# Five low weight parts made by ScalarE and an accumulating DMA in place of VectorE

## The chip, the cores and the metric

The kernel runs on one core of one Trainium2 chip. The metric is the device time of one execution in microseconds. The times of before are a median over 3 runs. Beside them stands one profiled execution, from which all rows below come.

## The reference, cut to what matters

The reference is a trunk of two layers over 512 tokens of width 1024. Layer 0 mixes with an S5 state-space layer, layer 1 with sparse attention, and each is followed by a SwiGLU feed-forward layer. The change lies in layer 0's mixer:

```
y = Re(C state) + D * u
y = gelu(y)
val, gate = split(y @ w_glu, 2)        # w_glu: 1024 x 2048
x = x + val * sigmoid(gate)
```

All of it is in float32. The kernel reaches this precision with three matmuls for each product: every operand is split into a rounded high part and a low part (the rest), and high times high, high times low and low times high are added in PSUM.

## The kernel before, in words

`wblock` fetches one block of weights: SP loads it to `w_raw` (line 262), ScalarE (ACT) copies it rounded to `w_hi` (line 263), and VectorE (DVE) writes the low part `w_lo` = `w_raw` - `w_hi` (line 265). `w_raw` has 2 buffers, `w_hi` and `w_lo` 3 each, shared by all layers.

The S5 layer works through its 64 channel groups in 8 rounds, `u` = 0 to 7. In a round VectorE makes tables (lines 666 to 671), the readout `VV` (lines 801 to 803, one buffer) and the scan with its rotations (lines 769 to 784, result `X`). TensorE (PE) transposes, and adds two products into `acc`: line 811, which needs `M` (filled from `Kd` by up to 8 small DMAs, line 717), and line 812, which needs `VV` and `X`. ACT applies GELU (line 817), PE transposes the result (line 825), and ACT and VectorE split it into the high and low part of `y[u]` (lines 830 and 831). GpSimd (POOL) only clears the first column of `X` in this stage (line 764).

Beside the rounds TensorE begins the projection `y @ w_glu` as a filler: 16 partial blocks (`glu_parts`, matmuls at lines 272 to 274 with high, high and low weights) take the `y[k]` that exist already. Every partial sum is copied out by ACT (`part`, line 873). The 16 blocks have 2, 2, 3, 3, 3, 3, 4, 4, 4, 4, 5, 5, 6, 6, 7 and 7 row tiles; neighbours are fetched together in 11 groups (`refill`). The first five groups hold two blocks each: 128x512, 128x768, 128x768, 128x1024 and 128x1024 elements. Groups 0 and 1 are fetched at the end of round 0. When all rounds are done, `glu_sum` computes the rest of the projection, and the feed-forward layer follows.

The order of each engine's instructions comes from a planner, which goes by program order as priority and by simulated readiness. Until the first `refill`, VectorE and ACT are under a manual schedule (line 432, closed at line 960). Each engine runs its instructions in the planned order, so an instruction that waits holds up those behind it.

Of the kernel before, what the change touches and what calls it, by code (L numbers as in the profile page):

```python
# [15 lines left out]
AF = mybir.ActivationFunctionType  # L16
ALU = mybir.AluOpType
# [3 lines left out]
P = 128  # L21
D = 1024
# [183 lines left out]
class Trunk:  # L206
# [47 lines left out]
    def wblock(self, src, nk, cols, lo_engine=None):  # L254

        nc = self.nc
        raw_t = self.wp.tile([P, KT * P], F32, name="w_raw", bufs=2)
        hi_t = self.wp.tile([P, KT * P], F32R, name="w_hi", bufs=3)
        lo_t = self.wp.tile([P, KT * P], F32R, name="w_lo", bufs=3)
        raw, hi, lo = (t[:, : nk * cols] for t in (raw_t, hi_t, lo_t))  # L260
        v = "p (k c) -> p k c"
        nc.sync.dma_start(out=raw.rearrange(v, k=nk), in_=src)
        nc.scalar.activation(hi, raw, AF.Copy)  # L263
        if lo_engine is None:
            nc.vector.tensor_tensor(lo, raw, hi, op=ALU.subtract)  # L265
        else:
            lo_engine.tensor_tensor(lo, raw, hi, op=ALU.subtract)  # L267
        return hi.rearrange(v, k=nk), lo.rearrange(v, k=nk)
# [98 lines left out]
    def s5(self, gain_row, x_ap, lre, lim, ldt, b_re, b_im, c_re, c_im, d_ap, w_glu):  # L367
        nc, tc = self.nc, self.tc
        V, PL, AC, PE = nc.vector, nc.gpsimd, nc.scalar, nc.tensor
        ident = self.ident  # L370
        wg = w_glu.rearrange("(k p) f -> p k f", p=P)
# [465 lines left out]
        cuts = [u for u in range(UN) for _ in range(GLU_BLOCKS[u])]  # L837
        cut.update(zip(order, cuts))
        groups, n = [], 0
        while n < len(order):  # L840
            m = n + 1
# [3 lines left out]
            n = m  # L845
        ready, done = {}, [0]
        fetched = [0]

        def refill(ahead):
            while fetched[0] < min(len(groups), done[0] + ahead):  # L850
                n, m = groups[fetched[0]]
                fetched[0] += 1
                d, i = order[m - 1]
                whi, wlo = self.wblock(wg[:, 0 : cuts[n], i * D + d * P : i * D + (d + m - n) * P], cuts[n], (m - n) * P)
                for b in range(n, m):
                    c = slice((m - 1 - b) * P, (m - b) * P)
                    ready[b] = whi[:, :, c], wlo[:, :, c]
# [67 lines left out]
        for u in range(UN):  # L925
# [30 lines left out]
            if more:  # L956
                ES[u + 1] = turns_out(u + 1, E[u + 1])
            refill(3 if u else 2)
            if u == 0:
                manual.close()  # L960
# [440 lines left out]
```

## Time and profile before

| | |
|---|---|
| median of 3 runs | 1294.6 us (1293.08 to 1294.64) |
| the profiled execution | 1290.61 us |
| its span, first to last instruction | 1288.9 us |
| mean granted TensorE clock | 0.993 |
| PE busy in the span | 1227.3 us (95%) |
| DVE busy | 764.7 us (59%) |
| ACT busy | 547.4 us (42%) |
| POOL busy | 147.9 us (11%) |

A share over the whole span is a mean over stages. The S5 rounds take about the first 186 us; the stage table among the rows below is the place to read for this change.

### The profile page before, as it was taken

The numbers are of one execution on the slowest core, as the hardware profiler recorded it, in microseconds if no ns is written. First come the engines' busy times: TensorE is split into PE (matmuls) and PEld (weight loads), VectorE is DVE, ScalarE is ACT, GpSimd is POOL, SyncE is SP. The second block draws the span as 40 slices with busy tenths as digits, with TensorE's granted clock in tenths as the row PEclk, the third lists the DMA queues.
The fourth block names the chain that finished last, engine by engine and source line by source line (L and its number), as shares of the span: only waits on it lengthen the run. The fifth ranks groups of instructions, "written<-read, shape, count | busy, mean of one in ns | idle before, by whom it ended". The sixth has DMA issues, their size and how long they took to land.

```text
span 1288.9 us, 18063 instructions
## 1 busy us (share of the span) xinstructions
PE 1227.3 (95%) x6844; PEld 1051.0 (82%) x6844; DVE 764.7 (59%) x1533; ACT 547.4 (42%) x1234; POOL 147.9 (11%) x174
## 2 busy tenths in 40 slices
PE   4589999999999999999989899999999999999998
PEld 4467778888888888889989799988888888888887
DVE  8999958654444443334899976775754444443221
ACT  7755445433332322322573778865532322232221
POOL 1000000000000000005754444510000000000000
PEclk9999999999999999999989999999999999999999
DMA  5021234333333333333213111111433333333341
GB/s 121 10 83 47 65 90 124 98 98 99 98 98 98 99 90 95 101 95 95 74 42 99 60 41 34 42 34 50 123 98 98 98 98 98 98 91 94 112 117 45
DMA packets 189735, 108.02 MB, mean 84 GB/s; under 512 B 7208, under 2 KB 188560, under 8 KB 189584
## 3 DMA queue, kind: packets, MB, share of 16 engines
q1 hardware_dynamic: 189264, 106.70, 28.5%
q8 instruction: 54, 0.88, 0.3%
q14 instruction: 33, 0.27, 0.1%
q10 hardware_dynamic: 384, 0.16, 0.1%
HBM read 102.39 MB, written 2.10 MB: 81 GB/s over the span
## 4 chain that ended last, share of the span: by engine, by line
PE 77%; DVE 5%; ACT 2%; issue 1%; DMA 1%; POOL 0%; ACTq 0%; DVEq 0%; POOLq 0%
PE acc L272 21%; PE acc L274 21%; PE acc L273 21%; PE acc L1062 8%; PE acc L1267 2%; PE tr L1256 1%; DVE ro L999 1%; PE lg L1240 1%; DVE pe L1243 1%; DVE mask L1170 1%; PE lg L1239 0%; DVE kl L1117 0%; PE tr L1099 0%; DVE m L1169 0%; ACT pe L1246 0%
## 5 line engine op out<-in xcount | busy, mean ns | idle before, releaser
L263 ACT ACTIVATE w_hi<-w_raw 128x1024 fp32r<-128x1024 f32 (+5 forms) x208 | 199.9, 963 | 512.9 <-PE acc L273 467.6
L265 DVE TENSOR_TENSOR w_lo<-w_raw,w_hi 128x1024 fp32r<-128x1024 f32 (+6 forms) x179 | 194.0, 1085 | 142.5 <-ACT w_hi L263 141.1
L272 PE MATMUL acc<-h,w_hi 128*128 128x512 f32 x704 | 274.5, 390 | 0.0
L274 PE MATMUL acc<-h,w_lo 128*128 128x512 f32 x704 | 273.9, 389 | 0.0
L273 PE MATMUL acc<-h,w_hi 128*128 128x512 f32 x704 | 273.7, 389 | 0.0
L1062 PE MATMUL acc<-w_hi,h 128*128 128x256 f32 (+1 forms) x896 | 174.7, 292 | 0.8 <-ACT h L284 0.8
L273 PEld LDWEIGHTS acc<-h,w_hi 128*128 128x128 f32 x704 | 132.2, 188 | 27.9 <-issue 0.5
L272 PEld LDWEIGHTS acc<-h,w_hi 128*128 128x128 f32 x704 | 132.2, 188 | 27.6 <-issue 0.5
L274 PEld LDWEIGHTS acc<-h,w_lo 128*128 128x128 f32 x704 | 132.2, 188 | 27.6
L1062 PEld LDWEIGHTS acc<-w_hi,h 128*128 128x128 f32 x896 | 141.4, 192 | 1.4 <-ACT h L284 1.0
L1062 PE MATMUL acc<-w_lo,h 128*128 128x256 f32 (+1 forms) x448 | 126.9, 288 | 0.3 <-POOL w_lo L267 0.3
L339 DVE TENSOR_TENSOR u<-acc,rinv 128x512 f32<-128x512 f32 x44 | 30.4, 690 | 132.4 <-PE acc L274 132.4
L272 PE MATMUL acc<-f,w_hi 128*128 128x512 f32 x272 | 106.4, 391 | 0.0
L274 PE MATMUL acc<-f,w_lo 128*128 128x512 f32 x272 | 105.9, 389 | 0.0
L273 PE MATMUL acc<-f,w_hi 128*128 128x512 f32 x272 | 105.8, 389 | 0.0
L1062 PEld LDWEIGHTS acc<-w_lo,h 128*128 128x128 f32 x448 | 85.2, 192 | 0.9 <-POOL w_lo L267 0.5
L336 DVE TENSOR_TENSOR g<-acc,rinv 128x512 f32<-128x512 f32 x44 | 30.4, 691 | 85.5 <-PE acc L274 85.5
L267 POOL TENSOR_TENSOR w_lo<-w_raw,w_hi 128x1024 fp32r<-128x1024 f32 (+2 forms) x29 | 69.5, 2408 | 49.9 <-ACT w_hi L263 49.8
L274 PEld LDWEIGHTS acc<-f,w_lo 128*128 128x128 f32 x272 | 51.1, 188 | 10.6
L273 PEld LDWEIGHTS acc<-f,w_hi 128*128 128x128 f32 x272 | 51.1, 188 | 10.5
L272 PEld LDWEIGHTS acc<-f,w_hi 128*128 128x128 f32 x272 | 51.1, 188 | 10.4
L272 PE MATMUL acc<-y,w_hi 128*128 128x512 f32 x128 | 51.1, 406 | 2.8 <-ACT y L830 1.1
(296 smaller groups left out, 1981.3 us busy)
## 6 DMA issues: line engine op xcount, KB each, us to landing
w_raw<-in_ffn_w_gate_up_dram SPq DMA_DIRECT2D x88, 512.0 KB, 3.7
w_raw<-in_ffn_w_down_dram SPq DMA_DIRECT2D x32, 448.0 KB, 3.7
w_raw<-in_dsa_w_in_dram SPq DMA_DIRECT2D x26, 512.0 KB, 3.5
w_raw<-in_ffn_w_down_dram SPq DMA_DIRECT2D x16, 512.0 KB, 3.8
w_raw<-in_dsa_w_o_dram SPq DMA_DIRECT2D x16, 256.0 KB, 2.8
w_raw<-in_s_w_glu_dram SPq DMA_DIRECT2D x6, 384.0 KB, 3.5
xc<-in_x_dram SPq DMA_DIRECT2D x8, 256.0 KB, 5.7
xr<-in_x_dram SPq DMA_DIRECT2D x4, 512.0 KB, 3.5
```

The lines of the kernel that those rows point to most:

```text
L263: nc.scalar.activation(hi, raw, AF.Copy)
L265: nc.vector.tensor_tensor(lo, raw, hi, op=ALU.subtract)
L267: lo_engine.tensor_tensor(lo, raw, hi, op=ALU.subtract)
L272: mm(out, lhsT=whi, rhs=xx[:, 0], start=start, stop=False)
L273: mm(out, lhsT=whi, rhs=xx[:, 1], start=False, stop=False)
L274: mm(out, lhsT=wlo, rhs=xx[:, 0], start=False, stop=stop)
L336: nc.vector.tensor_tensor(g, ps[0], rinv, op=ALU.mult)
L339: nc.vector.tensor_tensor(u, ps[1], rinv, op=ALU.mult)
L999: nc.vector.tensor_tensor(out, a, b, op=ALU.add)
L1062: PE.matmul(pt[:, :n], lhsT=h[k][:, l, ts], rhs=ww, start=(k == 0 and i == 0), stop=(k == KT - 1 and i == 2))
L1170: V.match_replace(out=sc, in_to_replace=m8, in_values=sc, imm_value=GONE)
L1267: PE.matmul(po[s, b][:, i * HD : (i + 1) * HD], lhsT=pT[:, j * P : (j + 1) * P], rhs=vv[j][:, (s * 4 + i) * HD : (s * 4 + i + 1) * HD], st ...
```

## The change

For the first five groups the low part is made in two steps in place of one. ACT writes minus the high part to `w_lo`, and a DMA that GpSimd issues adds the weights from DRAM to it. VectorE no longer takes part, and `w_raw` is read by ACT alone. The other six groups, `glu_sum` and the other layers keep the subtraction.

```diff
@@ wblock
         nc.scalar.activation(hi, raw, AF.Copy)
-        if lo_engine is None:
+        if lo_engine == "dma":
+            nc.scalar.activation(lo, hi, AF.Copy, scale=-1.0)
+            nc.gpsimd.dma_start(out=lo.rearrange(v, k=nk), in_=src, accum_op=ALU.add)
+        elif lo_engine is None:
             nc.vector.tensor_tensor(lo, raw, hi, op=ALU.subtract)
@@ refill
                 n, m = groups[fetched[0]]
+                lo = "dma" if fetched[0] < 5 else None
                 fetched[0] += 1
                 d, i = order[m - 1]
-                whi, wlo = self.wblock(wg[...], cuts[n], (m - n) * P)
+                whi, wlo = self.wblock(wg[...], cuts[n], (m - n) * P, lo)
```

## Rows read from the trace of the kernel before

**Rows 1.** Busy time (share of the span) and instructions of each engine, from the page

```profile
PE 1227.3 (95%) x6844; PEld 1051.0 (82%) x6844; DVE 764.7 (59%) x1533; ACT 547.4 (42%) x1234; POOL 147.9 (11%) x174
```

**Rows 2.** Windows: length, busy PE, PEld, DVE, ACT, POOL; PE clock; DMA share; GB/s

```profile
66.00:74.70 8.70, 7.73 (x68) 6.20 (x67) 8.64 (x16) 4.70 (x12) 0.00 (x0) 0.77 0.45 131
74.70:82.00 7.30, 6.01 (x61) 5.06 (x61) 7.27 (x15) 3.37 (x6) 0.00 (x0) 1.00 0.16 40
82.00:98.50 16.50, 13.95 (x113) 11.21 (x107) 16.41 (x31) 8.31 (x19) 0.11 (x1) 1.00 0.27 76
98.50:150.00 51.50, 51.10 (x376) 41.40 (x377) 50.84 (x96) 27.79 (x59) 0.33 (x3) 1.00 0.20 54
150.00:186.00 36.00, 33.99 (x242) 27.47 (x240) 22.18 (x39) 11.72 (x19) 0.52 (x3) 1.00 0.32 87
```

**Rows 3.** Timeline of DVE: start, duration, line, operation [idle before, releaser]

```profile
66.41 1.55 DVE L265 TENSOR_TENSOR w_lo<-w_raw,w_hi 128x512 fp32r<-128x512 f32 x2
67.88 0.68 DVE L771 TENSOR_TENSOR z<-z,z 128x512 f32<-128x512 f32 x1
...
77.01 0.95 DVE L265 TENSOR_TENSOR w_lo<-w_raw,w_hi 128x768 fp32r<-128x768 f32 x1
77.87 0.68 DVE L770 TENSOR_TENSOR z<-lg,ES 128x512 f32<-128x512 f32 x1
...
79.81 0.68 DVE L801 TENSOR_TENSOR VV<-Cst,hC 128x512 f32<-128x512 f32 x1
...
90.07 1.22 DVE L265 TENSOR_TENSOR w_lo<-w_raw,w_hi 128x1024 fp32r<-128x1024 f32 x1
91.20 1.72 DVE L784 TENSOR_TENSOR X<-z,z 64x252 f32<-64x252 f32 x4
...
104.96 1.22 DVE L265 TENSOR_TENSOR w_lo<-w_raw,w_hi 128x1024 fp32r<-128x1024 f32 x1
```

**Rows 4.** Timeline of PE around its idle gaps

```profile
72.22 0.62 PE L811 MATMUL acc<-M,U 128*64 128x128 f32 x4
...
73.34 0.40 PE L274 MATMUL acc<-y,w_lo 128*128 128x512 f32 x1
74.67 0.40 PE L812 MATMUL acc<-VV,X 128*64 128x128 f32 x2 [0.93 <-DVE X L784]
...
78.59 0.71 PE L825 MATMUL tr<-ident,yg 64*128 64x64 f32 x8 [0.68 <-ACT yg L817]
...
90.05 0.50 PE L272 MATMUL acc<-y,w_hi 128*128 128x512 f32 x1 [0.86 <-ACT part L873]
...
92.61 0.40 PE L812 MATMUL acc<-VV,X 128*64 128x128 f32 x2 [0.90 <-DVE X L784]
```

**Rows 5.** Timeline of ACT around the high parts

```profile
63.53 1.34 ACT L263 ACTIVATE w_hi<-w_raw 128x512 fp32r<-128x512 f32 x2
64.78 0.40 ACT L756 ACTIVATE ES<-E 128x256 f32<-128x256 f32 x1
...
66.78 0.60 ACT L680 ACTIVATE WT<-tr 128x512 f32<-128x512 f32 x1 [1.29 <-PE tr L679]
...
88.47 1.04 ACT L263 ACTIVATE w_hi<-w_raw 128x1024 fp32r<-128x1024 f32 x1
89.42 0.58 ACT L873 ACTIVATE part<-acc 128x512 f32<-128x512 f32 x1
```

**Rows 6.** DMA issues: count, size, median us to landing; and all loads to w_raw until 340 us

```profile
w_raw<-in_s_w_glu_dram SPq DMA_DIRECT2D x5, 256.0 KB, 2.6
w_raw<-in_s_w_glu_dram SPq DMA_DIRECT2D x6, 384.0 KB, 3.5
...
DMA to landing us min/median/max: 2.1/3.6/9.4
```

**Rows 7.** Timeline of SP and of POOL in the same stage

```profile
65.57 4.99 SPq L717 DMA_DIRECT2D M<-Kd  x8
...
84.72 0.11 POOL L764 MEMSET X<- 128x8 f32 x1 [22.35 <-DVE VV L803]
```

More of the change, by code (lines that the diff above doesn't have):

```diff
@@ L851, in refill @@
                 n, m = groups[fetched[0]]
+                lo = "dma" if fetched[0] < 5 else None
                 fetched[0] += 1
                 d, i = order[m - 1]
-                whi, wlo = self.wblock(wg[:, 0 : cuts[n], i * D + d * P : i * D + (d + m - n) * P], cuts[n], (m - n) * P)
+                whi, wlo = self.wblock(wg[:, 0 : cuts[n], i * D + d * P : i * D + (d + m - n) * P], cuts[n], (m - n) * P, lo)
                 for b in range(n, m):
```

## The prediction

> **What bounds the kernel now.** I read the page's busy times first: TensorE is busy for 95% of the span, VectorE for 59% [rows 1]. Read alone this says that VectorE's work is free. The change touches only the S5 rounds, so I asked next for the busy times stage by stage [rows 2]. From 66 to 98.5 us VectorE has no free time (8.64 of 8.70, 7.27 of 7.30, 16.41 of 16.50 us), while TensorE has gaps: 8.70 - 7.73 = 0.97, 7.30 - 6.01 = 1.29 and 16.50 - 13.95 = 2.55 us, 4.81 in all. From 98.5 to 150 us both engines are full: TensorE is idle for 0.40 us of 51.5. After 150 VectorE has 13.8 us to spare and TensorE 2.01. The reader should see that one stage has two regimes: what VectorE sheds before 98.5 us can move TensorE, what it sheds later can't, as TensorE is then full of its own work.
>
> Since the work of TensorE doesn't change, the kernel can become faster only by as much as its idle time shrinks. So the third view is TensorE's timeline with what ended each gap [rows 4]. Two of the large gaps wait for VectorE's `X`: 0.93 us before 74.67 and 0.90 us before 92.61. The others are a chain that leaves TensorE and comes back through ACT: 0.68 us for GELU's `yg` before 78.59, 0.86 us for a `part` copy before 90.05. VectorE isn't in these.
>
> **The change, part by part.** *Removed: five subtractions on VectorE* [rows 3]. The first row holds two of them (groups 0 and 1), and the next instruction starts 67.88 - 66.41 = 1.47 us later. Group 2 takes 77.87 - 77.01 = 0.86 us of the queue, groups 3 and 4 take 91.20 - 90.07 = 1.13 us each (the latter at 104.96). That is 1.47 + 0.86 + 2 x 1.13 = 4.59 us of VectorE.
>
> What of it reaches TensorE? The first `X` comes 1.47 us sooner, which is more than the gap of 0.93: TensorE goes on when its filler matmul of 73.34 ends, and gains 0.93. The second `X`, at 92.61, stands behind groups 0 to 3 and comes 1.47 + 0.86 + 1.13 = 3.46 us sooner, where TensorE needs it 0.93 + 0.90 = 1.83 sooner. So this gap goes too. The subtraction at 104.96 lies where TensorE is full [rows 2]; I cost it at nothing, and so the rest of the 3.46, which becomes slack of VectorE. Sum of this part: -1.83 us. Its bounds: the planner could leave one gap open where it is (-0.9), or use the freed VectorE to close every gap up to 98.5 us (-4.8).
>
> *Added: five negations on ACT.* They have the shapes of the high parts, so I take their price: the first two high parts take 64.78 - 63.53 = 1.25 us, one of 128x1024 takes 89.42 - 88.47 = 0.95 [rows 5]. Groups 0 and 1 then end on ACT at about 66.0, the two `ES` copies behind them at 66.7, and ACT waited until 66.78 for TensorE in any case: nothing, with 0.1 us of cover. At 88.47 it is tighter. The `part` copy of 89.42 ends the gap of 0.86 on TensorE, and a negation ahead of it would make that gap 0.95 us longer. The `part` copy stands earlier in program order than groups 3 and 4, which are fetched a round later, and so has the priority once both are ready. I take 0 and keep +0.95 for the range.
>
> *Added: five accumulating DMAs from GpSimd.* No row shows a DMA issued there, nor one that adds. Below, such a DMA can't take less than nothing; the plain loads to `w_raw` land 2.6 us (256 KB) and 3.5 us (384 KB) after issue, and the slowest load took 9.4 [rows 6]. An accumulate reads its destination as well, so I take twice the plain one: 5.2 us for group 0, with 2.6 and 9.4 as ends. Group 0 is needed first, by the matmul at 73.34 [rows 4]. If its negation follows its own high part, it ends about 64.7, and the data is there at 70 (67.3 to 74.1). The upper end is 0.8 us too late. The other groups have more room: group 1 was written by 67.9, and its matmuls can't begin before the two blocks of group 0 are done, the second of which is copied out at 89.42 [rows 5]; nearly 20 us. On GpSimd only the clearing of `X` stands behind these DMAs, 0.11 us at 84.72 after 22 us of waiting [rows 7]. Cost 0, upper end +0.8.
>
> *The collision.* Between 65.57 and 70.56 SP issues eight small DMAs that fill `M` [rows 7], and TensorE uses `M` at 72.22 [rows 4]. Groups 0 and 1 now put another 640 KB on the same DMA engines from about 65 on. In that window they are busy for 0.45 of their time, part of which is two loads behind the `M` DMAs [rows 2]. I expect the accumulates to be through before the last `M` transfer and take 0; the upper end is that `M` eats the first gain, +0.9.
>
> *Moved:* `w_raw` comes free after ACT's copy and not after VectorE's. The loads stand behind the `M` DMAs in SP's queue, so this gives nothing that TensorE would see. The 2 MB (256 + 2 x 384 + 2 x 512 KB) that are now read twice fall into stretches where the DMA engines are busy for 0.16 to 0.45 of the time [rows 2].
>
> **Sum.** 1290.6 - 1.83 = 1288.8 us for the profiled execution. The median of the runs shown is 4.0 us above that execution, for which I have no row; against the median the same sum gives 1294.6 - 1.8 = 1292.8 us. Case A's own range is -0.9 to -2.6, 1292.0 to 1293.7.
>
> **The rivals.** All differences under 0.2%, 2.6 us here, count as no change, as about what a measurement of this kernel can tell.
>
> *A, the forecast,* -1.8 us: the two `X` gaps close and no more. 46%.
>
> *B, the freed time closes other gaps too.* The order is planned anew, and with VectorE ahead by up to 3.5 us the filler matmuls could move into the gaps that wait for ACT. For it: most of 4.8 us is there. Against: those gaps are PE to ACT to PE, and the fillers themselves wait for `y[k]` and for weights. From -2.7 to -4.8; 32%.
>
> *C, the low part of group 0 is late, because GpSimd has no turn beside VectorE.* VectorE's instructions stand back to back [rows 2, 3]. If writing the DMA's descriptors has to wait for a pause of VectorE, then TensorE stands at 73.34 and with it the product of line 812 behind it, which frees `VV`; VectorE runs on until it needs that buffer, at 79.81 [rows 3], and only then pauses. 2.6 us for landing give 82.4: TensorE is 9.1 us late, about +8 us after the gain. It decides from a landing later than 73.34 + 0.93, the gap it may use up, and makes the kernel measurably slower from about 77.8 on. Against it: GpSimd's small operation at 84.72 takes 0.11 us in the middle of such a stretch [rows 7]. 8%.
>
> The Trainium skill, page "SBUF — State Buffer", section "Who interferes with whom", states this rule: a GpSimd-issued DMA has its descriptors written through a port pair that it shares with VectorE, and VectorE's copies and single-tensor operations in a two-port mode lock it out, while two-tensor operations take only the read side. By the lock the result would be that of C; by the exception, as VectorE's operations shown here are all two-tensor ones [rows 3], that of A. No run here shows such a DMA yet.
>
> *D, the new order costs more than it gives:* a negation ahead of a `part` or a `yg` copy at two or three places, 0.95 us each, and late `M` transfers. Two such places cancel the 1.8 us; with `M` and a third it is +1 to +4. Half of this still counts as no change: 14%.
>
> **How the numbers follow.** Faster by over 0.2%: B without its edge, and a small part of A, 0.33. Slower: C and nearly half of D, plus a few in a hundred for orders that I can't foresee, 0.18. Within 0.2%: the rest, 0.49. The range reaches down to 1289.3, all gaps up to 98.5 us and half a us of spread, and up to 1298.0, the middle of D's bad end; C's full price stays outside.
>
> **What would show it.** Right: no wait of TensorE for `X` near 74 and 92 us, VectorE's busy time down by about 5 us, ACT's up by some 4, the accumulates landing within 7 us, and TensorE's idle time from 66 to 98.5 us down from 4.8 to about 3. Wrong: TensorE waiting for a DMA of `w_lo` near 73 us or for `M` near 72; a new wait for `part`; idle time below 1.5 us there (B); or a kernel whose rounds end sooner and whose later stages give it back.

## The result and the profile after

The changed kernel is slower: 1302.7 us median of 6 runs (1301.53 to 1306.45) beside 1294.1 us for the kernel before on the same chip (1291.34 to 1294.64). The ratio of the mean times is 1.0076, 95% interval 1.0059 to 1.0093. The forecast was 1292.8 us with a range to 1298.0, so both the sign and the range were wrong. The profiled execution of after took 1301.53 us, with a span of 1299.8 us at a granted TensorE clock of 0.986. Behind the new lines of `wblock` its line numbers are those of before plus 3, behind `refill` plus 4; the experiments shift them by a few more.

The busy times on the page, to set beside [rows 1]:

```profile
PE 1233.2 (95%) x6844; PEld 1056.9 (81%) x6844; DVE 760.8 (59%) x1528; ACT 551.3 (42%) x1239; POOL 154.7 (12%) x179
```

VectorE lost 764.7 - 760.8 = 3.9 us and 5 instructions, ACT gained 3.9 us and 5 instructions. The work went where the change sent it, and nothing here explains 9 us. The same stretches as [rows 2] do (length, busy PE, PEld, DVE, ACT, POOL; clock; DMA share; GB/s):

```profile
66.00:74.70 8.70, 5.79 (x48) 4.66 (x48) 8.61 (x17) 6.43 (x13) 3.99 (x3) 0.50 0.93 210
74.70:82.00 7.30, 4.62 (x20) 4.06 (x20) 5.21 (x12) 1.02 (x4) 0.00 (x0) 0.50 0.67 138
82.00:98.50 16.50, 15.21 (x118) 12.22 (x116) 11.06 (x20) 8.48 (x19) 0.11 (x1) 0.90 0.07 16
```

From 66 to 82 us TensorE is idle for 2.91 + 2.68 us where it was 0.97 + 1.29. The DMA engines are busy for 0.93 of their time in place of 0.45, TensorE runs at the lower of its two clock levels (0.50, 1.2 GHz) throughout, and VectorE, which had no free time, is idle for 2.1 us of the second stretch. So round 1 is the place. Its length is read from one `y` to the next on ACT (line 830 before, 833 after): the `y` of rounds 0, 1, 2, 3 and 7 start at 61.48, 79.34, 97.28, 117.52 and 185.13 us before, and at 62.45, 88.78, 105.37, 126.64 and 194.87 us after. Round 1 takes 26.33 us in place of 17.86, which is 8.47 longer; round 2 is 1.35 shorter, round 3 is 1.03 longer; up to round 7 the sum is 8.8.

TensorE's timeline of round 1 after [rows 4]:

```profile
66.54 2.13 PE L682 MATMUL tr<-ident,W 128*128 128x128 f32 x8 [5.48 <-DVE Kd L717]
71.03 1.11 PE L623 MATMUL tr<-ident,xn 128*128 128x128 f32 x4 [2.37 <-ACT WT L683]
72.08 1.98 PE L693 MATMUL lg<-U,WT 128*64 128x64 f32 x32
73.98 3.62 PE L711 MATMUL tr<-Cz,W 128*128 128x32 f32 x16
80.28 1.12 PE L814 MATMUL acc<-M,U 128*64 128x128 f32 x4 [2.68 <-DMA M<-Kd]
...
82.91 0.69 PE L815 MATMUL acc<-VV,X 128*64 128x128 f32 x2
```

Two new waits stand there, 2.37 us for the `WT` copy and 2.68 us for `M`, and line 815 waits for `X` no more. In the trace of before neither wait exists, and the same rows are shorter:

```profile
67.47 1.07 PE L620 MATMUL tr<-ident,xn 128*128 128x128 f32 x4
68.47 1.81 PE L690 MATMUL lg<-U,WT 128*64 128x64 f32 x32
70.21 1.97 PE L708 MATMUL tr<-Cz,W 128*128 128x32 f32 x16
```

From the round's start to the first product of `M` it is 80.28 - 62.45 = 17.83 us after and 72.22 - 61.48 = 10.74 before: 7.09 more, of which the waits are 2.37 + 2.68 = 5.05 and the 16 matmuls of line 711 at the lower clock 3.62 - 1.97 = 1.65. From there to the next `y` it is 8.50 and 7.12: 1.38 more, though the 0.93 us wait for `X` has gone, since half of the products still run at the lower clock (0.63 us a pair in place of 0.38).

Where the two waits come from is read on SP, ACT and POOL [rows 5, 7]:

```profile
65.14 4.41 SPq L262 DMA_DIRECT2D w_raw<-in_s_w_glu_dram  x3
69.64 15.22 SPq L720 DMA_DIRECT2D M<-Kd  x16
```

```profile
66.54 0.84 ACT L265 ACTIVATE w_lo<-w_hi 128x768 fp32r<-128x768 f32 x1
68.31 0.84 ACT L263 ACTIVATE w_hi<-w_raw 128x768 fp32r<-128x768 f32 x1 [0.93 <-DMA w_raw<-in_s_w_glu_dram]
...
69.67 0.83 ACT L265 ACTIVATE w_lo<-w_hi 128x768 fp32r<-128x768 f32 x1
70.40 1.06 ACT L683 ACTIVATE WT<-tr 128x512 f32<-128x512 f32 x2
```

```profile
66.10 1.42 POOL L266 DMA_DIRECT2D w_lo<-in_s_w_glu_dram  x1 [2.76 <-ACT w_lo L265]
67.69 1.29 POOL L266 DMA_DIRECT2D w_lo<-in_s_w_glu_dram  x1 [0.17 <-issue]
70.80 1.28 POOL L266 DMA_DIRECT2D w_lo<-in_s_w_glu_dram  x1 [1.82 <-ACT w_lo L265]
```

The planner has turned both queues round. Before, SP issued the eight `M` DMAs from 65.57 to 70.56 and the next loads behind them. Now three loads stand ahead, and `M` begins at 69.64, though its source `Kd` was written by 66.48. On ACT the high part of group 2, whose load of 65.14 hasn't landed when ACT comes to it, and its negation stand ahead of the `WT` copies; `WT` starts at 70.40, where it started at 66.78. Then `M` is late on the way too. The landing of the five accumulates:

```profile
DMA to landing us min/median/max: 5.8/7.1/8.4
```

The last of the three loads, 512 KB for group 4, the eighth `M` transfer of round 1, what SP waited for ahead of it, and the landing of three `M` transfers of this round:

```profile
69.18 0.37 SPq L262 DMA_DIRECT2D w_raw<-in_s_w_glu_dram  x1
...
78.38 0.51 SPq L720 DMA_DIRECT2D M<-Kd  x1
```

```profile
SPq L720 <- DMA w_raw<-in_s_w_glu_dram: 3.9, 1, 3.9
```

```profile
M<-Kd SPq DMA_DIRECT2D x1, 64.0 KB, 1.9
M<-Kd SPq DMA_DIRECT2D x1, 56.0 KB, 6.2
...
M<-Kd SPq DMA_DIRECT2D x1, 48.0 KB, 6.6
```

The load issued at 69.18 takes 9.2 us to land (loads of this size from 60 to 110 us before: 3.9). The seven `M` transfers issued behind it, from 69.64 to 73.86, land 6.2 to 8.9 us after issue, from 78.5 on; the eighth, of 64 KB, waits on SP until that load has landed, is issued at 78.38 and lands 1.9 us later, at 80.28, when TensorE goes on. In the trace of before the eight transfers of this round land in 1.7 to 1.9 us. So `M` comes late because it stands behind the loads, and because these are slow beside the accumulates: the two loads of 512 KB take 8.0 us in the median here and 4.7 in e1 below, which has the loads in the same place and no accumulates.

### The profile page after: what moved, and what is told of

Same layout as the page of the kernel before. It is cut to its first block, busy times and chain, and to the rows that moved or that the text cites. A ratio compares the mean times of both kernels' runs of the same rounds, so it can differ in the third digit from the quotient of the medians.

```text
span 1299.8 us, 18068 instructions
## 1 busy us (share of the span) xinstructions
PE 1233.2 (95%) x6844; PEld 1056.9 (81%) x6844; DVE 760.8 (59%) x1528; ACT 551.3 (42%) x1239; POOL 154.7 (12%) x179
## 4 chain that ended last, share of the span: by engine, by line
PE 84%; DVE 5%; ACT 4%; DMA 3%; issue 1%; SPq 1%; POOL 0%; ACTq 0%; DVEq 0%; POOLq 0%
PE acc L275 22%; PE acc L276 22%; PE acc L277 21%; PE acc L1066 9%; PE acc L1271 2%; PE tr L1260 1%; PE acc L815 1%; PE acc L814 1%; PE tr L711 1%; DMA w_raw<-in_s_w_glu_dram 1%; SPq L720 1%; DMA craw<-in_s_c_im_dram 1%; PE lg L693 1%; PE lg L1244 1%; ACT xn L614 1%
## 5 line engine op out<-in xcount | busy, mean ns | idle before, releaser
L268 DVE TENSOR_TENSOR w_lo<-w_raw,w_hi 128x1024 fp32r<-128x1024 f32 (+6 forms) x174 | 189.2, 1087 | 146.5 <-ACT w_hi L263 145.2
```

## The experiments

**The theories.** *Order:* `w_raw` comes free without VectorE, so the planner puts loads ahead of `M` and group 2's high part ahead of `WT`. *Traffic:* the accumulates read 1 MB more in the window in which `M` travels, and `M` lands late. *ACT:* the negations themselves delay what stands behind them. *Clock:* a loss by TensorE's lower clock alone. In each table line the ratio is that of the mean times to the kernel before on the same chip, with its 95% interval; rounds are the distance of the `y` starts in the one profiled execution.

| kernel | median us | ratio | round 1, us | rounds 1 to 7, us |
|---|---|---|---|---|
| before | 1294.1 to 1295.2, by chip | 1 | 17.86 | 123.65 |
| after | 1302.7 | 1.0076 (1.0059 to 1.0093) | 26.33 | 132.42 |
| e1 | 1299.3 | 1.0029 (1.0017 to 1.0040) | 23.63 | 130.36 |
| e2 | 1300.7 | 1.0041 (1.0028 to 1.0055) | 21.62 | 130.51 |
| e3 | 1295.1 | 0.9998 (0.9990 to 1.0007) | 20.83 | 126.41 |
| e4 | 1296.7 | 1.0014 (1.0003 to 1.0024) | 17.88 | 124.49 |
| e5 | 1302.6 | 1.0065 (1.0052 to 1.0078) | 25.85 | 134.19 |
| e6 | 1299.9 | 1.0043 (1.0031 to 1.0055) | 19.20 | 128.43 |
| e7 | 1298.8 | 1.0029 (1.0018 to 1.0039) | 19.59 | 127.54 |
| e8 | 1306.4 | 1.0089 (1.0076 to 1.0102) | 19.48 | 130.39 |
| e9 | 1298.1 | 1.0032 (1.0019 to 1.0045) | 17.68 | 126.00 |
| e10 | 1296.5 | 1.0017 (1.0008 to 1.0026) | 16.70 | 124.85 |
| e11 | 1300.5 | 1.0053 (1.0039 to 1.0066) | 24.90 | 131.91 |
| e12 | 1298.6 | 1.0044 (1.0032 to 1.0057) | 17.99 | 126.17 |
| e13 | 1302.1 | 1.0056 (1.0043 to 1.0068) | 26.31 | 132.31 |
| e14 | 1294.9 | 1.0000 (0.9992 to 1.0009) | 17.86 | 124.03 |
| e15 | 1298.2 | 1.0016 (1.0005 to 1.0028) | 23.48 | 128.34 |

**e1: without the accumulating DMAs.** The low parts stay minus the high parts; the weights aren't added.

```diff
             nc.scalar.activation(lo, hi, AF.Copy, scale=-1.0)
-            nc.gpsimd.dma_start(out=lo.rearrange(v, k=nk), in_=src, accum_op=ALU.add)
```

> The change without its five DMAs from GpSimd: the low parts of the five groups stay at minus the high part, so the data lack the added weights. SP's order is that of the changed kernel (three loads to w_raw before the eight M transfers of round 1). Before is 1294.1 us, the change 1302.7. Theory Q (SP's new order alone does it: M issued late behind the loads, and the loads' own traffic): 1301 to 1303, M used by TensorE at 78 us or later. Theory T (the accumulates' traffic alone does it): 1292 to 1295, M used before 75. Both in part: 1296 to 1300.

A loss of 0.29% stays without any accumulate. SP's order is that of after (three loads, `M` from 70.22), TensorE waits 2.45 us for `WT`, and for `M` not at all: the transfers of round 1 land in 1.9 to 4.5 us.

**e2: the whole change, with `w_raw` held by VectorE.** VectorE reads 8 columns of it, so that it comes free when it did before.

```diff
             nc.gpsimd.dma_start(out=lo.rearrange(v, k=nk), in_=src, accum_op=ALU.add)
+            held = self.wp.tile([P, 8], F32, name="held", bufs=2)
+            nc.vector.tensor_tensor(held, raw[:, 0:8], hi[:, 0:8], op=ALU.subtract)
```

> The whole change, and in addition VectorE makes a subtraction on 8 columns that reads w_raw (about 0.1 us each), so that w_raw comes free as late as before; SP's order is then that of the kernel before (the eight M transfers before the two loads), with all five accumulates. Theory Q: the loss is gone, 1292 to 1295. Theory T: the loss stays, 1300 to 1303, with M landing 5 us or more after issue in round 1. Both in part: 1296 to 1300.

SP and TensorE of e2, round 1:

```profile
65.98 5.90 SPq L722 DMA_DIRECT2D M<-Kd  x8
71.98 1.07 SPq L262 DMA_DIRECT2D w_raw<-in_s_w_glu_dram  x2
```

```profile
74.36 1.09 PE L816 MATMUL acc<-M,U 128*64 128x128 f32 x4 [1.62 <-DMA M<-Kd]
```

The order of before is back and the wait for `WT` gone, yet `M` is still waited for: it lands in 1.7 to 4.9 us, median 3.4. A second stop stands in round 2, behind group 3's accumulate:

```profile
101.34 0.66 PE L816 MATMUL acc<-M,U 128*64 128x128 f32 x2 [3.14 <-issue]
```

The profile names no releaser for it, but the last `M` transfer of that round was issued at 96.1 and took 5.2 us to land, which makes 101.3. So the traffic costs by itself, 0.41%, and only a part of that in round 1. The two parts add up to 0.29 + 0.41 = 0.70% of the 0.76%, though in round 1 they aren't independent: `M`'s first product starts 17.83 us after the round's start in after and 12.48 us after it in e2.

**e3: ACT's part alone.** VectorE adds the weights to the negation.

```diff
-            nc.gpsimd.dma_start(out=lo.rearrange(v, k=nk), in_=src, accum_op=ALU.add)
+            nc.vector.tensor_tensor(lo, lo, raw, op=ALU.add)
```

> ACT writes minus the high part as in the change, and VectorE adds w_raw to it in place of the DMA: ACT's added work without any DMA, VectorE's work and SP's order as before. Theory A (the negations on ACT, ahead of the WT copies, cost): 1296 to 1299. Theories Q and T: as before, 1293 to 1296.

No difference, to within 0.1%. Five negations on ACT cost nothing in the order of before.

**e4 and e5: which groups.** `fetched[0] < 5` is replaced:

```diff
-                lo = "dma" if fetched[0] < 5 else None
+                lo = "dma" if fetched[0] in (3, 4) else None     # e4
+                lo = "dma" if fetched[0] < 3 else None           # e5
```

> The change for groups 3 and 4 alone; groups 0 to 2 by VectorE as before, and SP's order of round 1 is that of before. All theories that put the loss into round 1: 1293 to 1296, since the 2.26 us of VectorE that are saved lie where TensorE is nearly full, and M of a later round may come 1.4 us late. A theory of a cost per accumulate, wherever it is: 2/5 of the loss, 1297 to 1298.

> The change for groups 0 to 2 alone; groups 3 and 4 by VectorE. SP's order of round 1 is that of the change (loads before M). If the loss is made in round 1: that of the change less the 1.5 us that groups 3 and 4 alone cost, 1300 to 1302. If it were a cost of every accumulate: 3/5 of 7.5 us, 1299.5 or less.

Groups 0 to 2 carry nearly all of it (0.65%). Groups 3 and 4 alone cost 0.14%: in e4 a product of `M` late in round 2, at 99.31 and behind group 3's accumulate, waits 1.81 us for `M`; in after the first product of `M` behind that accumulate waits 1.42 us.

**e6: a plain load in place of the accumulate,** with `w_raw` held as in e2 and the subtraction back on VectorE (`lo` = `lo` - `hi`).

```diff
-            nc.gpsimd.dma_start(out=lo.rearrange(v, k=nk), in_=src, accum_op=ALU.add)
+            nc.gpsimd.dma_start(out=lo.rearrange(v, k=nk), in_=src)
+            held = self.wp.tile([P, 8], F32, name="held", bufs=2)
+            nc.vector.tensor_tensor(held, raw[:, 0:8], hi[:, 0:8], op=ALU.subtract)
+            nc.vector.tensor_tensor(lo, lo, hi, op=ALU.subtract)
```

> As the run with SP's old order and all accumulates (1300.7), but the five DMAs from GpSimd only load the weights over the negated high parts, and VectorE subtracts the high part afterwards: the same bytes at the same time, without adding in the DMA, and VectorE's work back. If the bytes on the shared DMA engines make M late: M waits by 1 us or more again, 1299 to 1302. If it is the adding: M lands within 2 to 3 us, no wait for M, 1294 to 1297.

`M` lands in 1.9 to 4.0 us, median 3.1 (3.4 in e2): the bytes slow it, whether added or only written. The plain loads from GpSimd land in 3.6 to 4.9 us, the accumulates of e2 in 4.3 to 6.5, so adding takes longer. In round 1 TensorE doesn't wait for `M` here, against what the first case expected; in round 2 it does, 2.60 us at 100.16. The total says less, since here VectorE waits 0.38 and 0.59 us for the plain loads, and TensorE then 1.78 us for `X`.

**e7 to e10 and e12: the same work earlier.** `refill(2)` is called some 20 us sooner in program order, so that the accumulates run before `M` travels. e7: groups 0 and 1 by accumulate, behind `normal(1)` (line 918 of before). e8: the same place, all by VectorE. e9: groups 0 to 2, same place. e10: groups 0 to 2, behind `spread(1)` (line 920). e12: e9's place, with GpSimd's subtraction in place of negation and accumulate.

```diff
         normal(1)
+        refill(2)            # e7, e8, e9, e12
         tokens(1)
         spread(1)
+        refill(2)            # e10
```

> Groups 0 and 1 fetched some 20 us sooner (a refill behind the second normal), where ACT waits for TensorE and the DMA engines are nearly idle from 46 to 60 us; their low parts by negation and accumulate as in the change, groups 2 to 4 by VectorE. If the change's idea holds and only its collision with M costs: no wait for M in round 1, X 1.5 us sooner, 1292 to 1294.5 against 1295.2. If the accumulate costs by itself: 1297 or more.

> The control of the run before: groups 0 and 1 fetched at the same early place, all low parts by VectorE. VectorE is full there, so I expect 1294 to 1296.5; the difference to the run before is what the two accumulates give, 1 to 2 us.

> Groups 0, 1 and 2 are fetched about 20 us earlier in program order, by ScalarE's negation and the accumulating DMA, so that the accumulates run before 60 us, where the DMA engines have time; groups 3 and 4 stay with VectorE. If the loss of the change came from the place of the accumulates and of the loads in the queue (my theory), M lands about 2 us after issue again and the kernel comes back to that before, or gains part of the 1.8 us of the two X gaps: 1292 to 1296. The run with two early groups gave 1298.8 since Kd came 2 to 3 us later; if early ScalarE work that delays Kd is what costs there, this one stays at 1298 or more.

> As the run before, with the early fetch put one step of the program elsewhere, behind a spread step rather than a normal step. If the place in the planner's order decides (Kd and the M transfers), this differs from it by 1 to 5 us in either direction with the same traffic; if the traffic decides, both give the same time within 1 us.

> The early fetch of groups 0 to 2 with GpSimd's subtraction in place of negation and accumulate. Against the early fetch with accumulates it tells what the second reading by DMA costs where DMA engines have time: the same within 1 us if nothing; GpSimd's passes of several microseconds lie beside work of 40 to 60 us, and low parts are needed only at 73 us. 1292 to 1297.

In none of e7, e9 and e10 does TensorE wait for `M` in round 1 (e7: 1.7 to 2.0 us to landing). Even so all three are slower than before: e7 waits 7.63 us for `Kd` ahead of round 1's transposes (5.29 before), and in e7 and e9 round 3 takes 24.35 and 24.34 us in place of 20.24. e8, e9 and e12 came out 9.9, 2.1 and 1.6 us above what was expected of them. e8 is no clean control: VectorE's early subtraction waits 4.46 us for ACT with all of VectorE's work behind it, and `y` of round 0 starts at 68.71 in place of 61.48. In e12 it starts at 65.83, so e12 against e9 doesn't tell what the second reading costs. e10 is nearest to what the forecast had in mind: no wait for `X` is left, and rounds 1 and 2 take 16.70 + 16.94 = 33.64 us, 2.16 less than the 35.80 of before. Round 3 gives it back, 23.82 us in place of 20.24, half of it by waits that weren't there before:

```profile
101.48 1.97 PE L711 MATMUL tr<-Cz,W 128*128 128x32 f32 x16 [1.02 <-ACT U L631]
105.44 0.80 PE L275 MATMUL acc<-y,w_hi 128*128 128x512 f32 x1 [0.98 <-ACT part L877]
```

The other half is work at a lower clock: TensorE is busy for 21.71 us in place of 19.91, with 145 matmuls in place of 143, and the granted clock is 0.79 from 102 to 108 us, where before has 1.00.

**e11: GpSimd subtracts,** with no second reading and no negation.

```diff
-                lo = "dma" if fetched[0] < 5 else None
+                lo = nc.gpsimd if fetched[0] < 5 else None
```

> No accumulating DMA and no negation: GpSimd makes the five subtractions, in the kernel before otherwise. VectorE sheds the same 4.59 us, nothing is read twice, and w_raw is held until GpSimd has read it. If only the queue order and the traffic cost in the change, this is 1293 to 1295; if GpSimd beside a full VectorE is slow (an elementwise pass of some microseconds on GpSimd), the low part of group 0 is late for the matmul at 73 us and it is 1296 to 1300.

Round 1 is as bad as in e1, and ACT and TensorE show why:

```profile
69.38 0.84 ACT L263 ACTIVATE w_hi<-w_raw 128x768 fp32r<-128x768 f32 x1 [4.38 <-DMA w_raw<-in_s_w_glu_dram]
70.13 1.07 ACT L683 ACTIVATE WT<-tr 128x512 f32<-128x512 f32 x2
```

```profile
70.76 1.11 PE L623 MATMUL tr<-ident,xn 128*128 128x128 f32 x4 [3.29 <-ACT WT L683]
```

ACT does no added work here. It stands still for 4.38 us at group 2's high part, with `WT` behind it, and TensorE waits 3.29 us. So the order costs without the change's own instructions.

**e13: 12 transposes put on TensorE** where it stands still in round 1 (work added, none removed).

```diff
-WARM = {}
+WARM = {1: 12}
```

> The whole change, with 12 transposes of the identity added on TensorE behind the lag products of round 1, where it stands still for WT and M: they add work and take none away. If the lower granted clock from 66 to 85 us is a part of the loss that follows from TensorE standing still, the clock rises sooner, y of round 1 follows y of round 0 by less than 26.3 us although 3 us of work were added, and the total falls by 1 to 3 us below 1302.7. If the clock is no more than a companion of the waits, the round gets as long or longer and the total is 1302 to 1306.

```profile
74.17 2.22 PE L899 MATMUL tr<-ident 128*128 128x128 f32 x12
76.22 1.87 PE L711 MATMUL tr<-Cz,W 128*128 128x32 f32 x16
80.48 1.11 PE L814 MATMUL acc<-M,U 128*64 128x128 f32 x4 [2.39 <-DMA M<-Kd]
```

With the transposes ahead of it, line 711 runs at the upper level (1.87 us in place of 3.62), but the first product of `M` starts 17.87 us after the round's start (17.83 in after), at the lower level again, and the round is as long as in after. Here too SP holds the eighth `M` transfer back behind the third load, for 3.3 us. So ahead of `M` it was the arrival of `M` that set the time, not the clock or the work of line 711. What the lower clock costs behind it this run didn't touch.

**e14 and e15: fewer groups.** e14 is group 2 alone. e15 is groups 1 and 2, with group 1's negation and accumulate written one round later in the program; the planner put them as early as in after all the same (issue at 67.05), so e15 is e5 with group 0 left to VectorE. Its lines that put group 1 off aren't shown.

```diff
-                lo = "dma" if fetched[0] < 5 else None
+                lo = "dma" if fetched[0] == 2 else None          # e14
+                lo = "dma" if fetched[0] in (1, 2) else None     # e15
```

> Only group 2 is made by negation and accumulating DMA; groups 0 and 1 stay with VectorE, which keeps the loads behind the M transfers, and 3 and 4 stay as well. If queue order and traffic beside the first M are the whole loss, it is gone: 1292.5 to 1295.5, at best 0.9 us faster by the second X gap. If any accumulate in this stage costs some microseconds, 1296 to 1299.

> Group 0 stays with VectorE; group 1's negation and accumulate are moved one round later, behind the first products of M; group 2 as in the change; 3 and 4 stay. VectorE sheds 0.9 us before the first X and 0.9 us more before the second. If the place of the traffic decides, M lands in about 2 us again, both X gaps shrink, and it is 1291.5 to 1294.5, a version that beats both kernels or equals that before. If group 2's load, which the trial order now puts four M transfers sooner, delays anything, 1296 or more.

With groups 0 and 1 left to VectorE the eight `M` DMAs come first again (e14, from 66.64), there is no wait for `WT` or `M`, and the loss is gone. The second wait for `X` is gone too; 0.9 us is less than this comparison can tell. In e15 one load gets ahead of `M`, SP's two rows being

```profile
65.88 0.40 SPq L263 DMA_DIRECT2D w_raw<-in_s_w_glu_dram  x1
66.52 5.28 SPq L726 DMA_DIRECT2D M<-Kd  x8
```

and with it group 2's high part ahead of `WT` on ACT:

```profile
68.97 0.84 ACT L264 ACTIVATE w_hi<-w_raw 128x768 fp32r<-128x768 f32 x1 [1.63 <-DMA w_raw<-in_s_w_glu_dram]
69.85 0.84 ACT L267 ACTIVATE w_lo<-w_hi 128x768 fp32r<-128x768 f32 x1
70.60 1.07 ACT L689 ACTIVATE WT<-tr 128x512 f32<-128x512 f32 x2
```

TensorE waits 2.53 us for `WT`, not for `M`, and round 1 takes 23.48 us. So in e1, e11 and e15 it is ACT's queue that costs, and no product waits for `M`; in after, with three accumulates beside it, `M`'s place behind three loads costs too. No kernel tried was faster than before.

## Why the prediction was wrong, by its own steps

*Removed, -1.83 us.* Right in place, not in effect. `X` is written by 74.5 us and neither `X` wait exists after. But in round 1 TensorE comes to `X` only at 82.91, so nothing was won there. Round 2 is 1.35 us shorter; how much of that is the saved work isn't shown, since VectorE also got ahead while TensorE stood still. The premise that TensorE's time can change only by its idle time failed as well, as the last point here shows. e10 shows that up to 2.16 us are to be had in the two rounds, and that the next round can take them back.

*Added on ACT, 0.* Right in the order of before: e3 gives 0.9998. In the order of after group 2's negation, 69.67 to 70.40, is 0.73 us of the wait for `WT`. The order of `part` and negation came out as argued.

*Moved, "this gives nothing that TensorE would see".* **This is the step that failed.** It took for given that the loads stand behind the `M` DMAs in SP's queue. That place was no property of the queue but the planner's answer to when `w_raw` came free. With VectorE out of it, the load of group 2 went ahead, and with it ACT's copy of that load went ahead of `WT`. e1, e11 and e15 each have that order and a wait for `WT` of 2.45, 3.29 and 2.53 us; e2, e3 and e14 have VectorE as a reader of the first two groups' `w_raw`, the order of before and no such wait. Price by e1: 0.29%.

*The collision, 0 with an upper end of +0.9 us.* Mis-sized. The landing time of group 0's accumulate was taken as 5.2 us (2.6 to 9.4) and measured 7.1, inside its bounds. What was left out is that three accumulates and three loads run in the same stretch: from 66 to 74.7 us the DMA engines went from 0.45 to 0.93 busy, and the `M` transfers of round 1 from 1.7 to 1.9 us to 6.2 to 8.9 for the first seven, with the eighth held back behind a load. The term was 0 to +0.9 us; TensorE's wait for `M` in round 1 measured 2.68 us, and 1.62 in e2, where the loads stand behind `M`. The prediction had named a wait for `M` as a sign of being wrong. The Trainium skill, page "DMA: Bandwidth & Descriptors", section "Issuing engines are not separate DMA queues", says that DMAs started by different engines run on the same 16 DMA engines and interleave. These rows agree. Price by e2, with all five accumulates: 0.41%.

*Rival C* is refuted. The three descriptor writes took 1.28 to 1.42 us while VectorE was busy for 8.61 of 8.70 us with two-tensor operations, and no product waited for `w_lo`. That is the exception of the Trainium skill's page "SBUF — State Buffer", section "Who interferes with whom", which the page itself calls inferred, as the prediction had read it.

*Rival D* named late `M` transfers and orders that cost, at +1 to +4 us. It had the right kind, but not the wait for `WT`, and at most half of the size measured: the two new waits of round 1 alone are 5.05 us.

*The 4.0 us between the profiled execution and the median,* for which the prediction had no row, go along with the granted clock. Over the first 22 runs of before beside the experiments, the one at 0.993 took 1290.96 us and the slowest, at 0.987, 1296.87. The same shows in round 1 of before, e3 and after (length, busy PE first, clock third from the end):

```profile
61.48:79.34 17.86, 12.13 (x104) 10.29 (x105) 17.77 (x34) 10.15 (x23) 0.11 (x1) 0.76 0.24 71
63.13:83.96 20.83, 16.06 (x104) 13.60 (x105) 20.34 (x39) 12.37 (x26) 0.11 (x1) 0.59 0.26 73
62.45:88.78 26.33, 16.52 (x104) 13.86 (x105) 18.77 (x38) 12.87 (x28) 4.10 (x4) 0.57 0.53 118
```

The same 104 matmuls keep TensorE busy for 12.13, 16.06 and 16.52 us. In e3, with no wait for `WT` or `M` and no loss in the median, round 1 is 2.97 us longer than in the profile of before, at a mean clock of 0.59 in place of 0.76. So up to some 3 us of the 8.47 in the two profiles can be this, and not the change. Against e3 the idle time of round 1 (4.77 us there) is 5.04 us longer in after, 2.45 in e1 and 1.62 in e2, which is what the new waits add up to in each. Most of the loss stays where the mean clock is alike: the seven of those 22 runs at 0.987 took 1295.1 to 1296.9 us, the four runs of after at 0.986 and 0.987 took 1301.5 to 1303.0. How much of the rest the lower clock adds to the waits stays open.

## What to carry to other kernels

When an edit takes away the last reader of a buffer, ask what the planner will do with the buffer that is free sooner, and check the order of the issuing queue and of the engine that reads the load next: a copy of data that is still on its way, put ahead of a copy that TensorE waits for, cost more here, 2.4 to 3.3 us of TensorE, than the 1.83 us that the saved VectorE time could give. Before adding DMA traffic, name the small transfers on which the bounding engine waits in the same few microseconds, add up all bytes of that window, not the one transfer by itself, and ask what stands ahead of them in their own queue. A gain of 1 to 2 us in one round counts only if the rounds behind it don't open new waits.

## What the runs showed of the hardware

An accumulating DMA issued by GpSimd took 5.8 to 8.4 us from issue to landing for 256 to 512 KB in after, 4.3 to 6.5 in e2, and 5.1 to 9.6 us for the first three groups in e10, where loads but no `M` transfer run beside it. In e2's place a plain load issued by GpSimd took 3.6 to 4.9 us (e6), and issuing it took GpSimd 0.74 to 0.96 us, where the accumulate took 1.28 to 1.42; SP's plain loads of 256 and 384 KB to `w_raw` took 2.6 and 3.5 us [rows 6]. In after, e5 and e13 the eighth `M` transfer behind a load was not issued before that load had landed: SP waited 3.9, 3.4 and 3.3 us. GpSimd's own subtraction is slow beside VectorE: 2.48 us for 128x512 and 6.22 us for two of 128x768 in e11, where VectorE takes 1.55 us for 128x512 and 128x768 together [rows 3]. The same 16 matmuls of line 711 took 1.97 us before, at a granted clock of 1.00, and 3.62 us in e3, at 0.50, with no wait ahead of them in either.
